# Attention weights of the whole prompt turned in 32 by 32 blocks on VectorE and put in place by SBUF transfers on two queues

## The chip, the cores and the metric

The kernel runs on one core of a Trainium2 chip. The metric is the device time of one execution in microseconds, lower is better. Every run is timed on the chip, and one more execution is recorded by the hardware profiler; all rows shown here come from that one.

## What is computed

The reference is one step of an encoder layer over a prompt of 2048 tokens and eight sample streams of 16 tokens each. One input projection feeds three branches (a gated convolution, a gated linear recurrence, an attention), and each branch goes through its slice of `w_branch`, is merged by gates and goes through `w_out`. The change touches the attention of the prompt alone. It has 8 heads of 64 channels and takes 128 queries at a time:

```python
def sb_attend(q, k, v, q_pos, k_pos):
    z = jnp.einsum('bqhd,bkhd->bhqk', qf, kf) * (1.0 / math.sqrt(SB_DH))
    causal = (k_pos[None, :] < q_pos[:, None])[None, None]
    log_1mb = jnp.where(causal, jax.nn.log_sigmoid(-z), 0.0)
    rest = lax.cumsum(log_1mb, axis=3, reverse=True) - log_1mb
    A = jnp.where(causal, jnp.exp(jax.nn.log_sigmoid(z) + rest), 0.0)
    return jnp.einsum('bhqk,bkhd->bqhd', A, vf)
```

A weight is the sigmoid of its own score times the product of (1 - sigmoid) over all keys between it and the query. The last product sums over keys, so the weights, which come out with queries on the partitions, have to be turned: keys on the partitions, queries along the row.

## The kernel before

Everything is float32 or a pair of float32 parts. The work has three stages. In the first (up to about 1340 us of the profile) the input projection of token groups 0 and 1 runs (matmuls L710 and L721), with the recurrence and the attention of the samples beside it. In the second (about 1340 to 2155 us) the projection of the third token group runs with the first part of the prompt's attention beside it. In the third (from about 2155 us) the branches are projected and merged (`bjob`, matmul L1440, the product with a gate on VectorE at L1446 and L1448, the sum at L1449), the output projection follows (`ojob`, L1471), and the rest of the prompt's attention runs beside that, up to about 2770 us.

The attention is a generator. It is advanced by a budget: each piece of foreground work names its cost in microseconds, that cost times a rate (0.65 in the second stage, 1.0 in the third) is credited, and every `yield` of the attention spends some of it. The merge of a group of 512 tokens calls `bg.drain(gi)` before it loads the attention's output, so what is left of that group's attention is then traced without foreground work between. The framework lays out each engine's queue from this order, and an instruction may be put ahead of one traced earlier; once laid out, each queue is worked off strictly in order.

The queries are taken in four blocks of 512 (`QBLOCKS`), the heads in four pairs. For a pair the keys are swept in segments of 512 from the newest to the oldest, once per head of the pair (`e` is 0 or 1). One such segment of one head is here called a sweep; there are 80. A sweep has four steps, one for each 128 queries (`i` from 0 to 3), 320 steps in all. A step is: two matmuls into `z` (L329, L330), two sigmoids on ScalarE (L333, L335) into `sn` and `sp`, a running product over the keys on VectorE (the scan, L342) into `pr`, and `sp` times `pr` (L347), which is the weight.

Three steps later (`DEPTH`) the helper `transposed` turns the weights: up to four 128 by 128 transposes on TensorE against the identity (L310) into the PSUM tile `tp`, and a copy by ScalarE (L311) into `aT`. When both heads of a segment are turned, `accumulate` adds `Vt` times `aT` into `pv` (16 matmuls, L359). After the last segment of a pair `store` multiplies by a gate (L366), splits the result into two parts and writes them to `OX` in DRAM (L182), from where the merge reads them (`load_o`, L1410).

`load_step` brings the keys `Kt` (two buffers) and the values `Vt` (two buffers). There is one buffer of `aT`, three of `sn`, four of `sp`, two of `pr`. All plain transfers are issued by SyncE (`nc.sync`), whose queue also carries the weights (`w`, `wst`: L208, L201), the gates of the merge (L1432, two buffers) and all stores.

## Time and profile before

| | us |
|---|---|
| median of 3 runs | 2874.01 |
| lowest and highest | 2873.08, 2874.37 |
| the profiled execution | 2876.11 |
| its span, first to last instruction | 2873.2 |

The granted TensorE clock was 1.0 throughout. The page gives busy time by engine, the chain of work that ended last, and groups of instructions: line, engine, operation, output and input, shape, count, then busy time and mean duration in ns, then the idle time of the engine just before them and what ended it. PE is TensorE's matmuls, PEld its weight loads, DVE is VectorE, ACT ScalarE, POOL GpSimd, SPq SyncE's queue of transfers. The view by windows gives the busy time and the number of instructions of each engine in a stretch, then the granted clock, the busy share of the 16 DMA engines and what they moved in GB/s. A TensorE that is listed as busy is not always at its peak, since matmuls are pipelined and their ends are modelled. The rows themselves stand in the prediction.

### The profile page before, as it was taken

Reading aid. Unit: us, or ns where it says so; the run is one execution under the profiler, and the core shown is the slowest. Engines: PE = TensorE matmul, PEld = TensorE weight load, DVE = VectorE, ACT = ScalarE, POOL = GpSimd, SP = SyncE. Lnnn points to the kernel's source line nnn. Section 1 sums busy time; section 2 is a strip of 40 time slices with the busy share of each in tenths; the row PEclk is TensorE's granted clock in tenths of the full one; section 3 lists DMA queues with packets and bytes.
Section 4 is the critical chain, followed back from the end, with each engine's and each line's share of the span. In section 5 each row is a group of like instructions: output and inputs, shape, how many; then the busy total and the mean of one; then the engine's idle time right before and its main releaser. Section 6 shows DMA issues by size and latency. Waiting matters only on the chain.

```text
span 2873.2 us, 51723 instructions
## 1 busy us (share of the span) xinstructions
PE 2853.0 (99%) x19479; PEld 2662.3 (93%) x19479; DVE 1546.5 (54%) x3304; ACT 1018.7 (35%) x2375; POOL 331.8 (12%) x802
## 2 busy tenths in 40 slices
PE   9999999999999999999999999999999999999999
PEld 9999999999999999999999999999998888787888
DVE  5454635641344442545434747557485876867743
ACT  4333222242233332213334444434444444544420
POOL 3110000111200000001323111111010011010100
PEclk9999999999999999999999999999999999999999
DMA  8887777777678887746766454544447877878876
GB/s 306 305 276 247 231 241 244 231 243 243 212 249 266 276 265 243 243 167 192 237 215 202 146 173 136 173 139 151 144 145 238 286 234 239 266 250 266 271 250 210
DMA packets 370475, 649.76 MB, mean 226 GB/s; under 512 B 33481, under 2 KB 246306, under 8 KB 339506
## 3 DMA queue, kind: packets, MB, share of 16 engines
q1 hardware_dynamic: 369458, 644.36, 68.2%
q8 instruction: 154, 2.52, 0.4%
q0 software_dynamic: 768, 2.10, 0.2%
q14 instruction: 95, 0.78, 0.1%
HBM read 447.06 MB, written 199.27 MB: 225 GB/s over the span
## 4 chain that ended last, share of the span: by engine, by line
PE 76%; DVE 2%; DMA 2%; issue 1%; ACT 0%; POOL 0%; SPq 0%; DVEq 0%; POOLq 0%; ACTq 0%
PE acc L710 33%; PE acc L721 10%; PE acc L1440 9%; PE acc L1471 6%; PE pv L359 4%; PE tp L310 4%; PE z L330 2%; PE z L329 2%; PE z L1039 1%; PE tp L458 1%; DMA gate<-GM 1%; PE pv L522 1%; PE z L476 0%; PE hg L1086 0%; PE hg L826 0%
## 5 line engine op out<-in xcount | busy, mean ns | idle before, releaser
L710 PE MATMUL acc<-hx,w 128*128 128x384 f32 (+1 forms) x6816 | 1251.8, 333 | 0.1
L710 PEld LDWEIGHTS acc<-hx,w 128*128 128x128 f32 x6816 | 1106.5, 188 | 21.9 <-issue 15.2
L721 PE MATMUL acc<-w,hx 128*128 128x256 f32 x2544 | 328.6, 284 | 1.8 <-DVE hx L176 0.9
L342 DVE TENSOR_TENSOR_SCAN pr<-snb,carry 128x513 f32<-128x513 f32 x192 | 246.5, 1284 | 153.3 <-ACT snb L333 151.7
L721 PEld LDWEIGHTS acc<-w,hx 128*128 128x128 f32 x2544 | 310.9, 188 | 5.0 <-DVE hx L176 1.7
L311 ACT COPY aT<-tp 128x512 f32<-128x512 f32 (+2 forms) x320 | 167.6, 524 | 375.2 <-PE tp L310 361.3
L710 PE MATMUL acc<-hx,wst 128*128 128x384 f32 x1248 | 247.2, 344 | 0.0
L1440 PE MATMUL acc<-o,w 128*128 128x512 f32 (+2 forms) x1080 | 234.7, 363 | 1.8 <-DMA o<-OX 1.8
L333 ACT ACTIVATE snb<-z 128x512 f32<-128x512 f32 (+2 forms) x320 | 172.4, 539 | 144.5 <-PE z L330 140.4
L710 PEld LDWEIGHTS acc<-hx,wst 128*128 128x128 f32 x1248 | 215.4, 188 | 6.4 <-issue 3.7
L1440 PEld LDWEIGHTS acc<-o,w 128*128 128x128 f32 x1080 | 185.1, 188 | 33.8 <-issue 5.3
L347 DVE TENSOR_TENSOR sp<-sp,pr 128x512 f32<-128x512 f32 (+2 forms) x320 | 195.3, 611 | 29.2 <-POOL sp L338 3.7
L342 DVE TENSOR_TENSOR_SCAN pr<-snb,one 128x129 f32<-128x129 f32 (+3 forms) x128 | 114.4, 894 | 123.9 <-POOL snb L338 123.6
L310 PE MATMUL tp<-idf,sp 128*128 128x128 f32 x1088 | 171.3, 273 | 2.5 <-ACT aT L311 1.5
L335 ACT ACTIVATE sp<-z 128x512 f32<-128x512 f32 (+2 forms) x320 | 171.5, 536 | 0.0
L1471 PE MATMUL acc<-w,mh 128*128 128x256 f32 x816 | 161.2, 285 | 1.0 <-DVE yt L1479 0.8
L1176 ACT ACTIVATE gm<-acc 128x384 f32<-128x384 f32 (+1 forms) x144 | 68.2, 474 | 230.4 <-PE acc L710 197.5
L310 PEld LDWEIGHTS tp<-idf,sp 128*128 128x128 f32 x1088 | 131.8, 141 | 19.3 <-issue 4.4
L176 DVE TENSOR_TENSOR w<-wst,w 128x1024 fp32r<-128x1024 f32 x72 | 88.1, 1223 | 110.7 <-ACT w L175 107.9
L1471 PEld LDWEIGHTS acc<-w,mh 128*128 128x128 f32 x816 | 131.0, 188 | 7.2 <-issue 4.2
L329 PE MATMUL z<-Kt,Q 128*128 128x512 f32 (+2 forms) x320 | 128.8, 403 | 0.3 <-ACT sp L335 0.2
L359 PE MATMUL pv<-aT,Vt 128*64 128x512 f32 (+3 forms) x640 | 128.1, 535 | 0.0
(299 smaller groups left out, 3570.1 us busy)
## 6 DMA issues: line engine op xcount, KB each, us to landing
w<-W SPq DMA_DIRECT2D x168, 1024.0 KB, 6.0
W<-w SPq DMA_DIRECT2D x72, 1024.0 KB, 5.0
wst<-W SPq DMA_DIRECT2D x112, 512.0 KB, 5.1
wst<-in_w_in_dram SPq DMA_DIRECT2D x72, 512.0 KB, 5.1
GM<-gm SPq DMA_DIRECT2D x120, 192.0 KB, 3.7
W<-mwp SPq DMA_DIRECT2D x40, 512.0 KB, 4.2
Kt<-KT SPq DMA_DIRECT2D x160, 128.0 KB, 3.1
o<-OX SPq DMA_DIRECT2D x72, 256.0 KB, 4.7
```

Source lines behind the costliest of these rows:

```text
L310: nc.tensor.transpose(tp[:, j * P:(j + 1) * P], sp[:, j * P:(j + 1) * P], idf)
L311: nc.scalar.copy(aT[:, e, 0:nb, i * P:(i + 1) * P], tp[:, :w].rearrange("p (b q) -> p b q", q=P))
L329: nc.tensor.matmul(z[:, :w], Q1[:, i * P:(i + 1) * P], Kt[:, :w], start=True, stop=False)
L333: nc.scalar.activation(sn[:, 512 - w:512], z[:, :w], AF.Sigmoid, scale=-0.125)
L335: nc.scalar.activation(sp[:, :w], z[:, :w], AF.Sigmoid, scale=0.125)
L342: nc.vector.tensor_tensor_scan(pr[:, 512 - w:513][:, ::-1], s_in, s_in, one if diag else carry[e][i], ALU.mult, ALU.bypass)
L347: nc.vector.tensor_tensor(sp[:, :w], sp[:, :w], pr[:, 513 - w:513], ALU.mult)
L359: nc.tensor.matmul(pv[64 * e:64 * e + 64, c0:n], Vt[:, j, e], aT[:, e, j, c0:n], start=first and j == 0, stop=last and j == nb - 1, skip_g ...
L710: nc.tensor.matmul(acc[:, :n], w[0][a][:, k], hT[b][:, k, :n], start=k == 0 and i == 0, stop=k == KB - 1 and i == 2)
L721: nc.tensor.matmul(acc[:, :256], hT[b][:, k, ti * P:(ti + 1) * P], w[k // 4][a][:, k % 4], start=k == 0 and i == 0, stop=k == KB - 1 and i ...
L1440: nc.tensor.matmul(acc[:, :n], w[0][a][:, k, dd * P:(dd + 1) * P], box[x][b][:, k, sl], start=k == 0 and i == 0, stop=k == 3 and i == 2)
L1471: nc.tensor.matmul(acc[:, :256], box["l" if b else "h"][:, k, ti * P:(ti + 1) * P], w[k // 4][a][:, k % 4], start=k == 0 and i == 0, stop= ...
```

## The change

The transposes on TensorE and the copies behind them are no longer called: `by_blocks` is set from the start and again before the third stage, so every sweep takes `turned_blocks`. One VectorE instruction per step turns each 32 by 32 block of the weights in its place, into a tile `T` of which there is one buffer, cleared once by GpSimd. After the last step of a sweep 16 transfers from SBUF to SBUF move the blocks to their partitions: each takes 32 partitions, and of each partition 16 runs of 32 values, in four runs of 512 bytes (64 KB in all). Eight are issued by SyncE and eight by ScalarE. They copy whole sweeps, so that blocks right of the diagonal go along. `aT` has a new order, in which the columns for `accumulate` are groups of 32 with a step of 128 values.

`accumulate` of a segment is held back in `pending` until the second step of the next segment's first sweep; at the end of a block of 512 queries it is held back by a `yield 5.0`. To make room, `sn` has two buffers in place of three, `Vt` one in place of two (its load moves behind the third step of the second head's sweep), and the tiles `ot` and `oth` of `store` share the two buffers of `pr`; the load of `ot` moves into the last `accumulate`.

```diff
-        for i in range(3):
+        for i in range(2):
             s = at.tile([P, 513], F32, name=f"snb{i}", bufs=1)
...
+        turned_.append(at.tile([P, 4, 4, 4, 32], F32, name="T", bufs=1))
+        nc.gpsimd.memset(turned_[0], 0.0)
...
-            nc.scalar.copy(aT[:, e, 0:nb, i * P:(i + 1) * P], tp[:, :w].rearrange("p (b q) -> p b q", q=P))
+            nc.scalar.copy(aT[:, e, i, :, 0:nb], tp[:, :w].rearrange("p (b a q) -> p a b q", a=4, q=32))
+
+        def turned_blocks(i, e, w, sp, aT):
+
+            T = turned_[0]
+            nc.vector.transpose(T[:, i, :, 0:w // P].rearrange("p c b q -> p b c q"),
+                                sp[:, :w].rearrange("p (b c q) -> p b c q", c=4, q=32))
+            if i == nq - 1:
+                for a in range(4):
+                    for c in range(4):
+                        queue_ = nc.scalar if (a + c) % 2 else nc.sync
+                        queue_.dma_start(aT[32 * c:32 * c + 32, e, :, a], T[32 * a:32 * a + 32, :, c])
...
-                aT = at.tile([P, 2, 4, 512], F32, tag="aT", name="aT", bufs=1)
+                aT = at.tile([P, 2, 4, 4, 4, 32], F32, tag="aT", name="aT", bufs=1)
+                turn_ = turned_blocks if by_blocks[0] else transposed
...
-                queue.append((True, lambda i=i, e=e, w=w, sp=sp, aT=aT: transposed(i, e, w, sp, aT)))
+                queue.append((True, lambda i=i, e=e, w=w, sp=sp, aT=aT, f=turn_: f(i, e, w, sp, aT)))
+                if e == 0 and i == 1:
+
+                    queue.extend(pending)
+                    pending.clear()
+                if e == 1 and i == 2:
+                    Vt = at.tile([P, 4, 2, 64], F32, tag="Vt", name="Vt", bufs=1)
+                    nc.sync.dma_start(Vt[:, :nb], VV[(1 + b0) * P:(1 + b1) * P, 2 * pair:2 * pair + 2].rearrange(
+                        "(b p) e c -> p b e c", p=P))
...
+                if last:
+                    gate.append(at.tile([P, 513], F32, tag="pr", name="ot", bufs=2))
+                    nc.sync.dma_start(gate[0][:, :n], SZ[pair][:, q0:q0 + n])
...
-                        nc.tensor.matmul(pv[64 * e:64 * e + 64, c0:n], Vt[:, j, e], aT[:, e, j, c0:n],
+                        nc.tensor.matmul(pv[64 * e:64 * e + 64, c0:n], Vt[:, j, e],
+                                         aT[:, e, c0 // P:nq, :, j].rearrange("p i a q -> p (i a) q"),
...
-            th = at.tile([P, 512], F32, tag="oth", name="oth", bufs=1)
+            th = at.tile([P, 513], F32, tag="pr", name="oth", bufs=2)
...
         yield from shorten(0)
+        if pending:
+            yield 5.0
+            queue.extend(pending)
+            pending.clear()
+            yield from shorten(0)
```

More of the change, by code (lines that the diff above doesn't have):

```diff
@@ L241, in trunk @@
     snb = []
+    turned_ = []
+    by_blocks = [True]
+    pending = []
     turn = [0]
@@ L317, in attn_pair @@
             load_step(m + 1)
-            if m == m1 - 1:
-                gate.append(at.tile([P, 512], F32, tag="ot", name="ot", bufs=1))
-                nc.sync.dma_start(gate[0][:, :n], SZ[pair][:, q0:q0 + n])
-            Q1, Q2, Kt, Vt = held[m]
+            Q1, Q2, Kt = held[m]
             nb = b1 - b0
@@ L324, in attn_pair @@
             if e == 0:
-                aT = at.tile([P, 2, 4, 512], F32, tag="aT", name="aT", bufs=1)
+                aT = at.tile([P, 2, 4, 4, 4, 32], F32, tag="aT", name="aT", bufs=1)
+                turn_ = turned_blocks if by_blocks[0] else transposed
+                if not by_blocks[0]:
+                    queue.extend(pending)
+                    pending.clear()
             for i in range(nq):
@@ L348, in attn_pair, with accumulate @@
                 yield 1.7 * w / 512
-                queue.append((True, lambda i=i, e=e, w=w, sp=sp, aT=aT: transposed(i, e, w, sp, aT)))
+                queue.append((True, lambda i=i, e=e, w=w, sp=sp, aT=aT, f=turn_: f(i, e, w, sp, aT)))
[6 more added lines that the diff above has]
+                        "(b p) e c -> p b e c", p=P))
                 yield from shorten(DEPTH)
-            def accumulate(nb=nb, diag=diag, first=si == 0, last=last, Vt=Vt, aT=aT):
+            def accumulate(nb=nb, diag=diag, first=si == 0, last=last, Vt=Vt if e else None, aT=aT):
                 if first:
                     box.append(ps_pv())
+                if last:
+                    gate.append(at.tile([P, 513], F32, tag="pr", name="ot", bufs=2))
+                    nc.sync.dma_start(gate[0][:, :n], SZ[pair][:, q0:q0 + n])
                 pv = box[0]
@@ L366, in store @@
             nc.vector.tensor_tensor(t[:, :n], box[0][:, :n], t[:, :n], ALU.mult)
-            th = at.tile([P, 512], F32, tag="oth", name="oth", bufs=1)
+            th = at.tile([P, 513], F32, tag="pr", name="oth", bufs=2)
             store_parts(OX[2, pair], slice(q0, q0 + n), t[:, :n], th[:, :n])
-        queue.append((False, store))
+        (pending if turn_ is turned_blocks else queue).append((False, store))
     queue = []
@@ L386, in attention @@
         yield from shorten(0)
+        if pending:
+            yield 5.0
+            queue.extend(pending)
+            pending.clear()
+            yield from shorten(0)
     def sample_attention():
```

11 lines of the change are left out of this document (3 added, 8 removed).

## The prediction

> **What bounds the kernel now.** I read the page's busy times first, then its chain.
>
> ```profile
> PE 2853.0 (99%) x19479; PEld 2662.3 (93%) x19479; DVE 1546.5 (54%) x3304; ACT 1018.7 (35%) x2375; POOL 331.8 (12%) x802
> ...
> PE 76%; DVE 2%; DMA 2%; issue 1%; ACT 0%; POOL 0%; SPq 0%; DVEq 0%; POOLq 0%; ACTq 0%
> PE acc L710 33%; PE acc L721 10%; PE acc L1440 9%; PE acc L1471 6%; PE pv L359 4%; PE tp L310 4%; PE z L330 2%; PE z L329 2%; PE z L1039 1%; PE tp L458 1%; DMA gate<-GM 1%; PE pv L522 1%; PE z L476 0%; PE hg L1086 0%; PE hg L826 0%
> ```
>
> TensorE is busy from end to end, and the chain lies on it. The transposes that the change removes (L310) hold 4% of it; no other engine has a share worth removing. But these are averages, so I asked the windows view for the stages.
>
> ```profile
> 0.00:1340.00 1340.00, 1331.64 (x9761) 1301.24 (x9762) 608.12 (x1618) 416.71 (x1003) 125.64 (x262) 1.00 0.75 246
> 1340.00:2155.00 815.00, 811.73 (x5277) 761.87 (x5276) 472.86 (x1028) 325.85 (x816) 147.47 (x341) 1.00 0.53 171
> 2155.00:2770.00 615.00, 610.98 (x3806) 509.65 (x3805) 429.92 (x600) 270.63 (x548) 58.71 (x199) 1.00 0.77 253
> 2770.00:2873.00 103.00, 98.62 (x643) 89.55 (x641) 35.57 (x60) 5.47 (x9) 0.00 (x0) 1.00 0.69 237
> ```
>
> The columns are PE, PEld, DVE, ACT, POOL, the clock, the share of the transfer engines and GB/s. The prompt's attention runs in the second and third rows. In the second, VectorE is busy 473 of 815 us and the transfer engines 0.53: room everywhere but on TensorE. In the third, VectorE is at 430 of 615 (0.70) and the transfer engines at 0.77. TensorE is still the bound there, but the two resources that the change loads are the next ones.
>
> **What is removed.** The chain asked stage by stage (second, then third):
>
> ```profile
> by line: PE acc L710 54.0%; PE acc L721 16.9%; PE pv L359 6.3%; PE tp L310 6.2%; PE z L330 3.5%; PE z L329 3.3%; PE z L1039 2.0%; DVE pr L342 0.8%; PE hg L826 0.6%; PE hg L1086 0.6%; DMA xt<-in_x_prompt_dram 0.6%; DMA Q<-QT 0.6%; PE tp L108
> by line: PE acc L1440 38.9%; PE acc L1471 23.1%; PE pv L359 11.8%; PE tp L310 10.4%; PE z L330 5.5%; PE z L329 5.4%; PE acc L710 1.6%; DMA o<-OX 0.8%; DMA GM<-gm 0.6%; issue 0.5%; DVE sp L347 0.2%; DVE mp L1449 0.1%; SPq L1410 0.1%; ACT snb
> ```
>
> 6.2% of 815 us is 50.5 us, 10.4% of 615 us is 64.0 us: 114.5 us of TensorE's path go if nothing takes their place. The busy time of the group is larger, since neighbours overlap in it:
>
> ```profile
> L311 ACT COPY aT<-tp 128x512 f32<-128x512 f32 (+2 forms) x320 | 167.6, 524 | 375.2 <-PE tp L310 361.3
> L310 PE MATMUL tp<-idf,sp 128*128 128x128 f32 x1088 | 171.3, 273 | 2.5 <-ACT aT L311 1.5 <-DVE sp L347 1.0
> ```
>
> 171.3 us is the upper bound of the saving, 114.5 the value I take. The copies on ScalarE (167.6 us) were hidden behind TensorE and are worth nothing by themselves.
>
> **What is added on VectorE.** 320 block transposes of one input and one output. No such instruction is in the trace. Nearest is the product of the same shapes (L347), an upper neighbour the scan (L342); per stage, product first:
>
> ```profile
> 1340.00:2155.00 815.00, 89.21 (x155) 1.00 0.53 171
> 2155.00:2770.00 615.00, 106.13 (x166) 1.00 0.77 253
> 1340.00:2155.00 815.00, 164.66 (x155) 1.00 0.53 171
> 2155.00:2770.00 615.00, 196.22 (x165) 1.00 0.77 253
> ```
>
> I take the product: 89 us in the second stage, 106 in the third; the bound above is the scan, 165 and 196, and a bound below half the product, 45 and 53, as it reads one input in place of two. VectorE then stands at 473 + 89 = 562 of 815, which hides, and at 430 + 106 = 536 us in the third stage. Without the transposes TensorE would need 615 - 64 = 551 us there, so VectorE would be at 97%. It cannot be hidden as before: with a short wait VectorE is the bound. Where foreground work on it is thickest (third branch of the merge) it has no gap already:
>
> ```profile
> 2473.32 1.28 DVE L342 TENSOR_TENSOR_SCAN pr<-snb,carry 128x513 f32<-128x513 f32 x1
> 2474.52 0.66 DVE L1448 TENSOR_TENSOR gate<-acc,gate 128x512 f32<-128x512 f32 x1
> 2475.10 0.68 DVE L347 TENSOR_TENSOR sp<-sp,pr 128x512 f32<-128x512 f32 x1
> 2475.70 0.68 DVE L1449 TENSOR_TENSOR mp<-mp,gate 128x512 f32<-128x512 f32 x1
> 2476.37 1.29 DVE L342 TENSOR_TENSOR_SCAN pr<-snb,carry 128x513 f32<-128x513 f32 x1
> 2477.57 0.67 DVE L176 TENSOR_TENSOR ml<-mp,mh 128x512 fp32r<-128x512 f32 x1
> ```
>
> The Trainium skill ("VectorE: DVE Perf Modes", section on the three transpose paths) gives 311 ns for a 128 by 128 bf16 turned on VectorE; four of them, as an estimate, make 1.24 us for a full step. No run here shows it yet; it would put the transposes at the scan's price, the fourth case below.
>
> **The wait that is added.** `T` has one buffer and all 16 transfers of a sweep read all of it, so the first transpose of the next sweep waits until the last has landed. Rows for issue and landing:
>
> ```profile
> 2472.43 2.34 SPq L1410 DMA_DIRECT2D o<-OX  x5
> Kt<-KT SPq DMA_DIRECT2D x160, 128.0 KB, 3.1
> OX<-ot SPq DMA_DIRECT2D x16, 256.0 KB, 2.0
> ```
>
> Five issues in a row take 2.34 us, 0.45 each; eight on each queue take 3.6 us. ScalarE's issues are not in the trace; I take SyncE's price, between nothing and twice that. Landing lies between 2.0 (a store) and 3.1 us (a load). So `T` is free 5.6 to 6.7 us after the sweep's last transpose. The next one comes one step later, in the third stage 615 us / 166 steps = 3.7 us. The wait is 1.9 to 3.0 us, per sweep (166 / 4 = 41.5 sweeps in the third stage, 155 / 4 = 39 in the second). Queued behind it on VectorE are the next scan and, in the merge, the products that empty `acc` (three buffers), for which TensorE waits. I take 1.9: 41.5 x 1.9 = 79 us, and 536 + 79 = 615 us. **The third stage then takes as long as before**, with VectorE in TensorE's place. The 64 us are given back.
>
> In the second stage a wait of 1.9 us x 39 = 74 us leaves VectorE at 636 of 765 us, so it mostly hides. What does not hide are the bursts: ScalarE waits for the last transpose and then issues for 3.6 us, and behind it stand the copies that empty `acc` (two buffers); SyncE does the same, and weights, keys and stores stand behind it. Between 0 and 1 us per sweep, I take 0.25: 10 us. Lifting the copies off ScalarE gives room for the 39 x 3.6 = 140 us of issues.
>
> **Transfers.** 16 x 64 KB is 1.05 MB per sweep, 43.5 MB in the third stage beside 253 GB/s x 615 us = 155.6 MB. The largest sustained flow of the page is 306 GB/s:
>
> ```profile
> GB/s 306 305 276 247 231 241 244 231 243 243 212 249 266 276 265 243 243 167 192 237 215 202 146 173 136 173 139 151 144 145 238 286 234 239 266 250 266 271 250 210
> ```
>
> 199.1 MB at 306 GB/s are 651 us, more than 615; but nothing in the trace says that 306 is a limit (TensorE was busy throughout there), and traffic inside SBUF leaves HBM alone. I cost it at nothing beyond the forecast's 615 us (324 GB/s) and keep 651 as a rival. The Trainium skill ("DMA: Bandwidth & Descriptors", section Measured) gives 0.95 us for 64 KB; 16 of them one after the other, as an estimate, are 15.2 us of the 14.8 us that a sweep takes. The rows above have larger transfers issued 0.45 us apart and landing in 2 to 5 us, so they overlap, and I do not take it.
>
> **Smaller edits.** `accumulate` waits for the landings, but is held back at least two steps (7 us), which covers 5.6 to 6.7: nothing. Its matmuls read groups of 32 in place of a plain row; no row has such an operand, so between nothing and as much again as it costs (4% of the chain, 115 us); I take nothing, as the count of columns is the same. The scans wait for `pr` while `ot` and `oth` hold it, 16 times, and the second `sn` is nearer; hidden behind foreground matmuls, up to 3 us each if not (48 us). Clearing `T` falls where GpSimd is idle.
>
> **The end.** The last attention output is read straight after it is written:
>
> ```profile
> 2764.73 4.39 PE L359 MATMUL pv<-aT,Vt 128*64 128x512 f32 x16
> 2770.53 0.32 SPq L182 DMA_DIRECT2D OX<-oth  x1
> 2773.56 0.88 SPq L1410 DMA_DIRECT2D o<-OX  x2
> ```
>
> So the last drain decides. Four `yield 5.0` put the attention 20 us of budget further back, and the last `accumulate` now waits 5.6 to 6.7 us for its transfers with nothing traced between. Merge matmuls that are left over cover part; I take 12 us, between 0 and 25.
>
> **The sum**, against the profiled execution of 2876.1 us (2.9 of it outside its span, 2.1 above the median of 2874.0): 2876.1 - 50.5 + 10 + 0 (third stage: -64 + 64) + 12 = 2847.6 us for the profiled execution, and 2.1 less, **2845.5 us**, for the median. I predict 2846.
>
> **The rivals.**
> First, *everything hides*: the wait on `T` falls into VectorE's gaps and only the end costs: third stage 551 us, 2876 - 114.5 + 10 + 12 = 2784. For it: the framework may put other work ahead of a waiting transpose. Against: the 97%.
> Second, *slower, by VectorE's wait on `T` in the third stage*: with landings like the loads' 3.1 us or later under load, the wait is 3 us and more: 536 + 41.5 x 3.0 = 661, +46 us, 2894; at 4 us 702 and 2935. It decides from 28 us over 615, a wait of 2.6 us. For it: VectorE without a gap; gates with two buffers, whose loads queue behind SyncE's bursts and which VectorE needs in order. Against: half of the stage (output projection, first branch) loads VectorE less.
> Third, *the transfers bound the third stage*: 651 us, +36: 2884. For it: share 0.77 before. Against: above.
> Fourth, *the transpose costs a scan*: 430 + 196 + 79 = 705 us, +90: 2938.
> Fifth, *no change*: the second stage's 40 us are eaten by bursts of 1 us and the drain: about 2874.
>
> **How the numbers follow.** Forecast (2800 to 2868) 0.45; everything hides (under 2800) 0.10; no change (2868 to 2880) 0.09; slower by the wait or the transfers (2880 to 2935) 0.29; dearer transposes or worse (above) 0.07. About 0.2% is what a measurement of this kernel can tell from no change. Faster 0.55, same 0.09, slower 0.36. The likeliest case's own range is 2800 to 2868; to leave out no more than 0.2 the range runs from 2782 to 2932.
>
> **What would show it.** Right: L310 and L311 gone; the second stage 40 us shorter; in the third VectorE above 0.85 busy, with waits of VectorE for landings into `aT` of about 2 us per sweep, and a chain with VectorE or transfers in it; the transposes near 0.69 us for 512 columns. Wrong: a third stage near 551 us (everything hid), one over 640 us (waits or transfers), transposes of 1.2 us, L359 dearer, or transfers that land in more than 4 us.

## The result, and the profile after

| | before | after |
|---|---|---|
| median, us | 2874.19 | 3169.43 |
| lowest to highest of 4 runs each | 2873.08 to 2875.68 | 3157.35 to 3179.72 |
| the profiled execution | 2876.11 | 3168.90 |
| its span | 2873.2 | 3167.2 |
| mean granted TensorE clock | 1.000 | 0.956 |

The changed kernel takes 1.1025 times as long, with a 95% interval of 1.0986 to 1.1065: 295 us slower. The forecast was 28 us faster, and the time lies far above its range.

From the page of the kernel after: busy time by engine, the granted clock in 40 slices, and the two groups of instructions that the change adds or alters.

```profile
PE 2902.5 (92%) x18391; PEld 2625.5 (83%) x18391; DVE 1691.7 (53%) x3623; ACT 874.3 (28%) x2055; POOL 337.2 (11%) x803
...
PEclk9999999999999999999999999999988888888899
...
L316 DVE STREAM_TRANSPOSE T<-sp 128x512 f32<-128x512 f32 (+2 forms) x320 | 186.1, 608 | 49.2 <-DMA aT<-T 47.5
L382 PE MATMUL pv<-aT,Vt 128*64 128x512 f32 (+3 forms) x640 | 166.1, 553 | 31.1 <-DMA aT<-T 29.9
```

No engine is full any more. TensorE went from 99% to 92%, VectorE stands at 53%. TensorE's instructions fell by 1088, the transposes, and yet its busy time rose by 50 us: in the last third the granted clock drops, and each matmul lasts longer. So the time was not lost to more work. It was lost to waiting, and to the lower clock that goes with it.

Where it was lost is read from two instructions that bound the stages: the first matmul of the merge on `o`, with which the third stage begins, and the last matmul of `accumulate`, with which the attention ends. The view by source line gives the first and the last start of each, here for before and for after:

```profile
L1440 PE MATMUL acc<-o,w x1080: 274/392/483, 2182.9 to 2816.5; 128*128 128x512 f32 x108, 128*128 128x384 f32 x38, 128*128 128x256 f32 x34
L359 PE MATMUL pv<-aT,Vt x640: 272/592/644, 1385.9 to 2768.5; 128*64 128x512 f32 x112, 128*64 128x384 f32 x16, 128*64 128x256 f32 x16, 128*64 128x128 f32 x16
...
L1470 PE MATMUL acc<-o,w x1080: 274/392/796, 2195.0 to 3109.6; 128*128 128x512 f32 x108, 128*128 128x384 f32 x36, 128*128 128x256 f32 x36
L382 PE MATMUL pv<-aT,Vt x640: 272/592/1116, 1395.7 to 3078.9; 128*64 128x512 f32 x112, 128*64 128x256 f32 x26, 128*64 128x384 f32 x16, 128*64 128x128 f32 x6
```

The second stage thus ends 12.1 us later (2195.0 - 2182.9), the third takes 883.9 in place of 585.6 us, 298.3 more, and what comes after it is 16.4 us shorter (88.3 in place of 104.7 of the span). That makes the 294 us between the spans. **The third stage holds nearly all of the loss.** The shorter end is no gain of its own: of the 2528 matmuls of the merge and the output projection 376 start after the attention's last matmul in the trace of after, where 496 did before, so 120 of them have moved into the third stage.

The windows view of after for the second and the third stage, columns as in the prediction:

```profile
1340.00:2195.00 855.00, 806.16 (x4878) 733.27 (x4878) 537.11 (x1189) 259.66 (x677) 142.51 (x343) 0.99 0.71 211
2195.00:3075.00 880.00, 681.46 (x3227) 519.37 (x3228) 514.75 (x766) 190.45 (x365) 66.81 (x197) 0.86 0.76 226
```

In the third stage TensorE is busy for 77% at a clock of 0.86, VectorE for 58%, the transfer engines for 0.76 at 226 GB/s, less than the 253 GB/s before. Nothing is saturated. Both parts of the loss can be read against the run without transfers that is told below (`no_transfers`: 563.3 us busy of 588 for 3206 matmuls): TensorE's matmuls take 118 us longer in after, and it stands idle for 174 us more (198.5 in place of 24.7). What VectorE and ScalarE wait for in that window (engine, line, what released it; then us in total, times, longest):

```profile
ACT snb L345 <- DMA aT<-T: 87.1, 15, 9.4
ACT sp L347 <- DMA aT<-T: 80.1, 11, 9.7
DVE gate L1478 <- DMA gate<-GM: 46.9, 25, 5.4
DVE mp L1476 <- DMA gate<-GM: 35.4, 14, 7.7
DVE T L316 <- DMA aT<-T: 32.0, 15, 3.8
PE pv L382 <- DMA aT<-T: 28.0, 15, 3.7
ACT sp L347 <- DMA o<-OX: 24.8, 3, 10.3
DVE yt L1509 <- DMA xr<-in_x_prompt_dram: 21.0, 14, 4.9
DVE yt L1509 <- DMA out_dram<-yt: 18.6, 8, 5.5
```

The wait that the prediction priced, VectorE's for `T` (L316), is one of the small ones: 32 us. Larger are waits for things that the change did not touch: the gates (82 us in two rows) and the rows of `x` for the output, all of them loads by SyncE. And ScalarE waits 167 us for landings in `aT` before its sigmoids (two rows), though a sigmoid reads and writes nothing of `aT`, and 25 us for `o`, which it does not read either. Such a row says that something else, which stood ahead of the sigmoid in ScalarE's queue, had to wait. A stretch of the timeline shows it (start, duration, engine, operation; in brackets the idle time before and what ended it):

```profile
2862.57 7.81 SPq L322 DMA_DIRECT2D aT<-T  x8
...
2864.15 3.92 ACTq L322 DMA_DIRECT2D aT<-T  x4
...
2868.11 0.62 ACT L175 CAST mh<-mp 128x512 fp32r<-128x512 f32 x1 [3.35 <-DMA aT<-T]
...
2870.48 0.53 SPq L1462 DMA_DIRECT2D gate<-GM  x1
```

SyncE needs 7.8 us for its eight issues, waits between them included, and the load of the next gate stands behind them until 2870.5. ScalarE needs 3.9 us for four, and a cast (L175) that makes the merge's operand for TensorE stands behind those. The view of `aT` has the issues by queue (duration min, median and max in ns, first and last start):

```profile
L322 ACTq DMA_DIRECT2D aT<-T x640: 592/612/1935, 1353.6 to 3072.8; - x160
L322 SPq DMA_DIRECT2D aT<-T x640: 585/603/2244, 1355.2 to 3073.4; - x160
```

So one of these issues takes 0.6 us, 640 times on each of two queues that have other work: 640 x 0.603 = 386 us of SyncE and 392 us of ScalarE, to replace 168 us of copies on ScalarE.

### The profile page after: what moved, and what is told of

It is laid out like the page before. It is cut to its first block, busy times and chain, and to the rows that moved or that the text cites. A ratio compares the mean times of both kernels' runs of the same rounds, so it can differ in the third digit from the quotient of the medians.

```text
span 3167.2 us, 51219 instructions
## 1 busy us (share of the span) xinstructions
PE 2902.5 (92%) x18391; PEld 2625.5 (83%) x18391; DVE 1691.7 (53%) x3623; ACT 874.3 (28%) x2055; POOL 337.2 (11%) x803
## 5 line engine op out<-in xcount | busy, mean ns | idle before, releaser
L1470 PE MATMUL acc<-o,w 128*128 128x512 f32 (+2 forms) x1080 | 256.2, 389 | 46.6 <-DVE gate L1478 18.6
L1470 PEld LDWEIGHTS acc<-o,w 128*128 128x128 f32 x1080 | 201.3, 207 | 95.5 <-DVE gate L1478 24.4
L316 DVE STREAM_TRANSPOSE T<-sp 128x512 f32<-128x512 f32 (+2 forms) x320 | 186.1, 608 | 49.2 <-DMA aT<-T 47.5
L1501 PE MATMUL acc<-w,mh 128*128 128x256 f32 x816 | 180.5, 311 | 34.5 <-DVE yt L1509 16.6
L382 PE MATMUL pv<-aT,Vt 128*64 128x512 f32 (+3 forms) x640 | 166.1, 553 | 31.1 <-DMA aT<-T 29.9
L1501 PEld LDWEIGHTS acc<-w,mh 128*128 128x128 f32 x816 | 149.0, 216 | 43.0 <-DVE yt L1509 19.2
L341 PEld LDWEIGHTS z<-Kt,Q 128*128 128x128 f32 x320 | 62.3, 195 | 105.6 <-ACT sp L347 83.9
L382 PEld LDWEIGHTS pv<-aT,Vt 128*64 128x64 f32 x640 | 53.0, 139 | 105.1 <-issue 89.7
```

What stands on the lines that cost most here:

```text
L316: nc.vector.transpose(T[:, i, :, 0:w // P].rearrange("p c b q -> p b c q"), sp[:, :w].rearrange("p (b c q) -> p b c q", c=4, q=32))
L341: nc.tensor.matmul(z[:, :w], Q1[:, i * P:(i + 1) * P], Kt[:, :w], start=True, stop=False)
L382: nc.tensor.matmul(pv[64 * e:64 * e + 64, c0:n], Vt[:, j, e], aT[:, e, c0 // P:nq, :, j].rearrange("p i a q -> p (i a) q"), start=first an ...
L1470: nc.tensor.matmul(acc[:, :n], w[0][a][:, k, dd * P:(dd + 1) * P], box[x][b][:, k, sl], start=k == 0 and i == 0, stop=k == 3 and i == 2)
L1501: nc.tensor.matmul(acc[:, :256], box["l" if b else "h"][:, k, ti * P:(ti + 1) * P], w[k // 4][a][:, k % 4], start=k == 0 and i == 0, stop= ...
```

## The experiments

The theories:
- **T wait**: VectorE waits for the landings before it writes `T` again (the prediction's second rival).
- **Bytes**: the transfers fill the transfer engines (its third).
- **Loop**: the transfers wait until `accumulate` has read `aT`, `accumulate` and all behind it on TensorE wait for the transfers.
- **Issues**: 16 issues per sweep hold SyncE's and ScalarE's queues, and the loads, casts and sigmoids behind them come late.

Each time is that of one execution; the kernel before, run beside them on the same chip, took 2872 to 2876 us. The four runs of after spread over 22 us, so smaller differences among the slow kernels are not told apart. The table has all kernels, in the order in which they are told. "Third stage" is from the first merge matmul on `o` to the last matmul of `accumulate`, read as above.

| kernel | us | third stage begins | its length | granted clock, whole run |
|---|---|---|---|---|
| before | 2876.1 | 2182.9 | 585.6 | 1.000 |
| after | 3168.9 | 2195.0 | 883.9 | 0.956 |
| buffers_only | 2877.5 | 2185.1 | 587.1 | 0.999 |
| no_transfers | 2808.9 | 2136.3 | 588.0 | 0.997 |
| second_only | 2913.5 | 2197.9 | 621.4 | 0.994 |
| third_only | 3139.8 | 2186.6 | 854.0 | 0.960 |
| const_source | 3144.0 | 2168.2 | 883.8 | 0.957 |
| quarter_bytes | 3114.9 | 2193.2 | 827.6 | 0.965 |
| quarter_count | 2899.2 | 2143.2 | 671.2 | 0.988 |
| sp_pool | 3088.3 | 2186.0 | 812.6 | 0.967 |
| sp_queue | 3335.8 | 2299.4 | 945.5 | 0.941 |
| pool_queue | 3288.4 | 2277.6 | 932.2 | 0.947 |
| by_dram | 3127.2 | 2168.6 | 880.5 | 0.966 |
| by_dram_second | 2891.9 | 2173.5 | 624.1 | 0.995 |
| sink | 3146.9 | 2182.8 | 855.3 | 0.960 |
| const_sink | 3103.6 | 2178.0 | 814.0 | 0.960 |
| const_sink_pool | 2969.3 | 2212.4 | 670.3 | 0.978 |
| const_sink_act | 2885.3 | 2212.4 | 587.1 | 0.991 |
| const_sink_sp | 3008.1 | 2153.3 | 753.5 | 0.975 |
| rows | 3142.4 | 2193.5 | 858.0 | 0.957 |

### What the side edits cost, and what could be won

`buffers_only` keeps all the buffer edits and the new order of `aT`, but turns the weights on TensorE as before.

```diff
-    by_blocks = [True]
+    by_blocks = [False]
...
-    by_blocks[0] = True
```

> The weights are turned by TensorE throughout as before, with everything else of the change: two sn buffers, one Vt, ot and oth in the buffers of pr, aT in the new order. If the loss comes from the transfers or the wait on T: within 15 us of 2874. If it comes from the smaller buffers: over 3000. If the new order of aT makes the accumulate matmuls dearer: 20 to 115 us over 2874, with their mean above 535 ns.

2877.5 beside 2875.4 us: two sigmoid buffers, one `Vt`, shared `pr` tiles and the strided operand of `accumulate` cost about 2 us together. They are not the cause.

`no_transfers` turns the blocks into `T` as in the change, but moves nothing; `accumulate` reads a cleared `aT`.

```diff
...
-                for a in range(4):
-                    for c in range(4):
-                        queue_ = nc.scalar if (a + c) % 2 else nc.sync
-                        queue_.dma_start(aT[32 * c:32 * c + 32, e, :, a], T[32 * a:32 * a + 32, :, c])
+                pass
...
-                aT = at.tile([P, 2, 4, 4, 4, 32], F32, tag="aT", name="aT", bufs=1)
+                aT = turned_[1]
```

> Leaves the 16 transfers of every sweep out (accumulate reads a tile of zeros, so the attention's output is left out of the result); the block transposes on VectorE, their buffers and the held back accumulate stay. If the wait on T, the issues or the bytes of the transfers are the cause of the loss (three theories that this run doesn't tell apart), TensorE's saving shows and the time is 2780 to 2830 us, with the clock back at 1.0. If VectorE's 186 us of transposes alone fill the third stage, 2850 to 2950. If the smaller buffers are the cause, over 3000.

2808.9 us, 66.5 us below the run beside it. Its windows, second stage and third:

```profile
1340.00:2136.00 796.00, 784.03 (x4890) 726.05 (x4889) 549.38 (x1196) 263.02 (x680) 138.04 (x343) 1.00 0.55 178
2136.00:2724.00 588.00, 563.30 (x3206) 455.00 (x3206) 502.43 (x760) 181.94 (x360) 62.26 (x195) 0.99 0.81 266
```

The second stage ends 46.6 us earlier than before (2182.9 - 2136.3). The third takes 588 us, as long as before, though it has fewer matmuls and no landing in `aT` to wait for: VectorE is busy for 502 of 588 us there (0.85), TensorE for 563 (0.96), and the chain has both. What follows it is 21.9 us shorter (82.8 in place of 104.7), with 102 fewer matmuls of the merge and output projection left in it. Third stage and end together are thus 19.5 us shorter (670.8 in place of 690.3). So all that the transposes could give is these 66 us, 46.6 of them in the second stage, and **the transfers take away 360 us** (3168.9 - 2808.9). The experiments that follow ask how.

### One stage at a time

`second_only` turns by blocks in the second stage alone, `third_only` in the third alone: of the two switches shown above one is set to `False`, ahead of the third stage or at the start.

> Turned in blocks in the second stage, by TensorE in the third. The second stage of the changed kernel took 855 us in place of 815: if the stages are independent, 2874 + 40 = 2914, 2890 to 2940. If the second stage's loss came from attention that the third left over or the other way round, the sum of this run's and the next one's excess differs from 295 us by more than 40.

> Turned by TensorE in the second stage, in blocks in the third, which took 880 us in place of 615 in the changed kernel: if the stages are independent, 2874 + 255 = 3129, 3090 to 3160, with a clock of about 0.86 in the third stage. My forecast's own wait on T (1.9 to 3.0 us a sweep) would give 2874 to 2925.

+38 us (2913.5 beside 2875.4) and +264 us (3139.8): together 302, the change's own loss of 295 within a few us. The stages lose on their own. Nor does the second stage alone win anything: in `second_only` its end is at 2197.9 in place of 2182.9, where without transfers it was 46.6 us early. It also leaves work behind: 164 scans in place of 157 start in the third stage, 8 of its block transposes among the work left over, and that stage is 36 us longer than before.

### Is it the wait on T, the bytes, or the count?

`const_source` lets the transfers read a constant tile, so that VectorE never waits for them before it writes `T`. `quarter_bytes` keeps the 16 transfers and moves one of a sweep's four steps (16 KB in place of 64). `quarter_count` issues 4 of the 16, of 64 KB each. In both of these `aT` is one tile that is cleared at the start, as in `no_transfers`.

```diff
 const_source
-  queue_.dma_start(aT[32 * c:32 * c + 32, e, :, a], T[32 * a:32 * a + 32, :, c])
+  queue_.dma_start(aT[32 * c:32 * c + 32, e, :, a], g_bc[32 * a:32 * a + 32, 0:512].rearrange("p (i r) -> p i r", i=4))
 quarter_bytes
+  queue_.dma_start(aT[32 * c:32 * c + 32, e, 0, a], T[32 * a:32 * a + 32, 0, c])
 quarter_count
-                    for c in range(4):
-                        queue_ = nc.scalar if (a + c) % 2 else nc.sync
+                    for c in (a,):
+                        queue_ = nc.scalar if a % 2 else nc.sync
```

> All 16 transfers per sweep, full size, into aT as before, but read from a constant tile in place of T; VectorE still turns every step into T, so T is never read, no transpose waits for a landing and no issue for a transpose (the attention's weights are left out of the result). Theory of the wait on T, my forecast's: 2810 to 2860, since the wait is gone. Issue theory (issues take ScalarE's and SyncE's time, and each waits for an earlier transfer's completion): still over 3000. Bytes theory: over 3000.

> All 16 transfers per sweep are issued, but each moves one run of 512 bytes per partition in place of four (16 KB in place of 64 KB); the rest of aT stays zero, so three quarters of the attention's weights are left out. Without any transfers the kernel took 2809 us, with all 3169: 360 us to explain. Bytes theory (the transfer engines are full): a quarter of 360, about 2900. Issue theory (number of transfers, their place in the queues and their completion): 3080 to 3170. Theory of the wait on T: landings are a little shorter, 3050 to 3150.

> Four full transfers of 64 KB per sweep, two on each queue, in place of 16; the other blocks of aT stay zero, so three quarters of the weights are left out. Same bytes as in the run with a quarter of the bytes. Bytes theory: the same time as that run, about 2900. Issue theory: 2820 to 2890, clearly under that run. Wait on T: T is free about 1.2 + 2.6 = 3.8 us after the last transpose, so hardly a wait: 2810 to 2850.

3144.0, 3114.9 and 2899.2 us. Without the T wait 25 us come back of 360, hardly more than the runs of after differ among themselves, with a quarter of the bytes 54, with a quarter of the issues 270 (9 us less than the issue theory had expected at the least). **The price goes mainly by the transfer, not by the byte, and VectorE's wait is a small part of it.** The third stage makes a near straight line of it. The transposes L316 in its window are 168, so 42 sweeps of four; with 0, 4 and 16 transfers per sweep it takes 588.0, 671.2 and 883.9 us. That is 83.2 / 168 = 0.50 us per transfer for the first four, and 295.9 / 672 = 0.44 us over all 16, beside an issue of 0.60 us.

### Other queues

`sp_pool` issues ScalarE's eight on GpSimd, `sp_queue` all 16 on SyncE, `pool_queue` all on GpSimd.

```diff
-                        queue_ = nc.scalar if (a + c) % 2 else nc.sync
+                        queue_ = nc.gpsimd if (a + c) % 2 else nc.sync    # sp_pool
+                        queue_ = nc.sync                                  # sp_queue
+                        queue_ = nc.gpsimd                                # pool_queue
```

> The changed kernel with ScalarE's eight transfers per sweep issued by GpSimd in place of ScalarE. Issue theory: ScalarE's queue is free and GpSimd's transfers complete on their own, 2880 to 3000, if GpSimd needs no more than about 1 us for each issue (8 per sweep of 14 us); if it needs more, T is free later and the time rises to 3100 or more. Wait on T: 3100 or more in any case, as the last landing isn't earlier. Bytes: unchanged, 3150 to 3190.

> All 16 transfers per sweep issued by SyncE, none by ScalarE. If ScalarE's blocked queue (sigmoids behind issues) is the larger part: 2950 to 3080, though SyncE then issues 9.6 us per sweep. If SyncE's blocked queue (gates, weights and keys behind issues) is the larger part: over 3200.

> The changed kernel with all 16 transfers per sweep issued by GpSimd: SyncE's and ScalarE's queues are as without them, and GpSimd's transfers have completion semaphores of their own. The issues took 0.55 us each there, 8.8 us per sweep of 14, so T is free only about 12 us after the last transpose and the wait on T grows. If SyncE's and ScalarE's blocked queues are what costs: 2900 to 3020. If the length of the path from T to accumulate is what costs: over 3150.

3088.3, 3335.8 and 3288.4 us. With ScalarE freed 81 us come back, which lies between the two ranges that had been expected (2880 to 3000, and 3100 or more). SyncE alone is worst. `pool_queue` is a miss: it frees both engines and was to come out at 2900 to 3020 us. Its waits in the third stage show what replaced the old ones:

```profile
ACT sp L347 <- DVE T L316: 400.6, 49, 21.1
...
PE pv L382 <- DMA aT<-T: 160.4, 27, 11.3
...
POOL aT L322 <- PE pv L382: 93.3, 14, 12.9
POOL aT L322 <- DVE T L316: 90.0, 20, 15.2
```

With one queue the last of 16 issues comes at least 16 x 0.55 = 8.8 us after the first (the view of `sp_pool` has 0.55 us for one on GpSimd), `accumulate` and the next `T` wait for it, and GpSimd, standing at an issue that waits for `accumulate` (93 us), holds up the masks and carries of the next scan: in the same view the scans wait 60 us for these two (37.2 and 22.5). Here the loop does seem to cost. This left two theories, loop and issues, for the change itself.

### Fewer and larger transfers by way of DRAM

`by_dram` writes `T` to DRAM in one transfer of SyncE and reads it back in four of GpSimd; `by_dram_second` does so in the second stage alone and transposes on TensorE in the third.

```diff
+                TD = dram.tile([P, 4, 4, 4, 32], F32, tag="TD", name="TD", bufs=2)
+                nc.sync.dma_start(TD, T)
+                for c in range(4):
+                    nc.gpsimd.dma_start(aT[32 * c:32 * c + 32, e].rearrange("p i a j q -> p i a (j q)"),
+                                 TD[:, :, c].rearrange("(a r) i b q -> r i a (b q)", a=4))
```

> In place of 16 transfers inside SBUF, five per sweep through DRAM: T is written whole by SyncE (1 MB in rows of 8 KB), and four reads by GpSimd bring it back in runs of 512 bytes. Twice the bytes, a third of the issues, one of them on SyncE, and T waits for one landing alone. Issue theory: 2830 to 2920. Bytes theory: the third stage carries 2 x 43.5 MB more, over 3050.

> The same five transfers per sweep in the second stage alone, TensorE's transposes in the third, where VectorE would become the bound even without transfers (588 us before, 590 without transfers). The second stage saved 47 us without transfers: 2874 - 47 + up to 30 for the five issues and the longer path = 2830 to 2860, faster than both kernels. Bytes theory: 2890 or more.

3127.2 and 2891.9 us: neither is in the range of the issue theory, both are in that of the bytes. The windows row of `by_dram`'s third stage, the row of its reads (KB each, us to landing), the issue of its write and the longest wait of GpSimd's issues there:

```profile
2168.00:3049.00 881.00, 690.12 (x3291) 515.99 (x3293) 510.24 (x772) 188.94 (x363) 212.70 (x367) 0.88 0.94 285
...
aT<-TD POOLq DMA_DIRECT2D x320, 256.0 KB, 7.6
...
L320 SPq DMA_DIRECT2D TD<-T x80: 319/325/752, 1355.8 to 3011.4; - x80
...
POOL aT L322 <- DMA TD<-T: 206.3, 20, 19.7
```

The transfer engines stand at 0.94, and a read lands after 7.6 us. But a share of 0.94 is not by itself the reason: `const_sink_pool`, told below, has it too in a third stage of 670 us. The path also got longer, as a read waits for the write to land: GpSimd stood 206 us at such issues in that stage. Which of the two costs, bytes or path, was not separated, so these two runs say little about the change's own loss.

### Cutting the loop

`sink` lets `accumulate` read a constant tile in place of `aT`: nothing on TensorE waits for a transfer. `const_sink` does that and lets the transfers read a constant tile as well: no instruction waits for a transfer's data and no transfer for an instruction; what is left are the issues, their bytes and their completions. `const_sink_pool` is `const_sink` with all issues on GpSimd.

```diff
 sink, const_sink, const_sink_pool
-                                         aT[:, e, c0 // P:nq, :, j].rearrange("p i a q -> p (i a) q"),
+                                         g_bc[:, c0:n],
```

> Leaves out: accumulate reads a constant tile in place of aT, so nothing on TensorE waits for the 16 transfers of a sweep and the transfers wait for no matmul; they still read T, and VectorE still waits for them before it writes T again. If the cost is the closed loop (b): about 2830 to 2900 us, that is 270 us and more come back. If it is the issues on ScalarE and SyncE (a): 3050 to 3150 us, near the 3144 us of the constant source.

> Leaves out: the transfers carry a constant tile to aT and accumulate reads a constant tile, so no instruction waits for a transfer's data and no transfer for an instruction; only the 16 issues of a sweep, their bytes and their completions are left, at the same places of ScalarE's and SyncE's order. (b) the closed loop: 2810 to 2860 us, as without any transfer (2809). (a) the issues by themselves: 3050 us or more. In between (2900 to 3000): both, in the share that it shows.

> As const_sink, with all 16 issues on GpSimd in place of ScalarE and SyncE. By (a), the issues hold ScalarE's and SyncE's queues: 2810 to 2860 us, as these are free of them, and TensorE waits little for GpSimd. If the transfers cost by what they do in the transfer engines, whoever issues them: within 40 us of const_sink.

3146.9 and 3103.6 us: the loop theory, which had 2830 to 2900 and 2810 to 2860, falls. **Of the 360 us, 295 are there with nothing but the issues** (3103.6 - 2808.9). (These issues still carry their bytes, and each has a landing that is reported.) Closing either half of the loop adds some 40 (to 3144.0 with `accumulate` waiting, to 3146.9 with `T`), both halves 65. ScalarE in `const_sink` (timeline):

```profile
2420.28 5.45 ACTq L322 DMA_DIRECT2D aT<-g_bc  x5
2425.82 0.60 ACT L345 ACTIVATE snb<-z 128x512 f32<-128x512 f32 x1 [5.91 <-DMA aT<-g_bc]
```

The sigmoid has no tie to these transfers; it waits 5.9 us because five issues stand ahead of it, from the first to the last 5.45 us. Each of the five takes 0.59 to 0.61 us in its own record, 3.0 together; in the 2.5 us between them an issue waits in its turn. With all issues on GpSimd the price is 160 us over `no_transfers` in place of 295, 134 less, and yet 2969.3 lies well above the 2810 to 2860 expected. That it matters which queue is held is likely, but this run doesn't show it alone: 886 of its 1280 issues start before the third stage, where `const_sink` has 665, so that 394 are left for the third stage in place of 608.

### Whose queue?

`const_sink_act` and `const_sink_sp` are `const_sink` with only one queue's eight transfers. In `rows` the tiles are laid out so that a transfer moves one run of 2 KB per partition in place of four of 512 bytes.

```diff
 const_sink_act
+                        if (a + c) % 2 == 0:
+                            continue
+                        queue_ = nc.scalar
 const_sink_sp
+                        if (a + c) % 2:
+                            continue
+                        queue_ = nc.sync
 rows
...
-            nc.vector.transpose(T[:, i, :, 0:w // P].rearrange("p c b q -> p b c q"),
+            nc.vector.transpose(T[:, :, i, 0:w // P].rearrange("p c b q -> p b c q"),
...
-                        queue_.dma_start(aT[32 * c:32 * c + 32, e, :, a], T[32 * a:32 * a + 32, :, c])
+                        queue_.dma_start(aT[32 * c:32 * c + 32, e, a], T[32 * a:32 * a + 32, c])
...
```

> As const_sink (constant source, accumulate reads a constant), with only ScalarE's 8 transfers of a sweep; SyncE's 8 are left out. If the cost is each queue's own issue time, the two halves add up to const_sink's 295 us over 2809, with the larger part here, since the sigmoids stand behind these issues: about 2980 to 3010 us, and 2880 to 2910 for SyncE's half. If it is the shared limit on transfers under way, each half costs much less than half: 2820 to 2870 us here, and the two halves together under 100 us.

> As const_sink, with only SyncE's 8 transfers of a sweep; ScalarE's 8 are left out. Own issue time: 2880 to 2910 us, the rest of the 295 us. Shared limit on transfers under way: 2820 to 2870 us.

> Leaves nothing out. T and aT are laid out so that a transfer moves one run of 2 KB per partition in place of four of 512 bytes, the count and the bytes unchanged. If the pieces of a transfer set the price (its issue or its landing): issues under 0.5 us, landings nearer 2.0 us, and 3000 us or less. If the price is per transfer: issues of 0.6 us as before and 3110 to 3180 us.

3008.1 us with SyncE's half, 2885.3 with ScalarE's: 199 and 76 us over `no_transfers`, 275 of `const_sink`'s 295 together. SyncE's half is by far the dearer; I had expected the opposite. But the two are not alike, as the view of `aT` in `const_sink_act` shows:

```profile
L324 ACTq DMA_DIRECT2D aT<-g_bc x640: 592/612/2267, 1332.7 to 2213.9; - x160
```

With nothing to wait for, the framework put all but 2 of ScalarE's 640 issues ahead of the third stage, and the second stage gets 76 us longer (2212.4 - 2136.3); the third takes 587 us. So this run says what ScalarE's issues cost in the second stage when there are twice as many, and nothing of the third. There `const_sink`, with 304 of ScalarE's issues beside SyncE's, takes 60.5 us more than SyncE's alone (814.0 - 753.5).

`const_sink_sp` spreads its issues over both stages like the change (1355 to 2908 us). It costs 17 us in the second, **165 us in the third stage** (753.5 - 588.0) and 17 behind it. The chain of work there:

```profile
2690.27 0.70 DVE mp L1481
2690.99 0.32 SPq L1464
...
2691.36 0.64 SPq L324
...
2695.95 0.60 SPq L324
2696.59 0.59 SPq L201
...
2698.26 0.50 SPq L293
...
2700.60 0.43 SPq L1442
2701.07 8.15 DMA o<-OX
2709.28 5.43 DMA gate<-GM
```

SyncE itself lies on the chain: from 2691.4 to 2696.5 us it issues eight transfers into `aT`, behind them come weights (L201), keys (L293) and `o` (L1442). Then the issue of a gate stands until an `o` has landed (8.15 us), with which it shares no data, and the landing of the gate ends the wait at 2714.7. So the issues of the burst are 5.2 us of this piece, and the larger part are landings that follow late. VectorE's waits in that stage:

```profile
DVE gate L1480 <- DMA gate<-GM: 34.9, 14, 8.3
...
DVE yt L1511 <- DMA xr<-in_x_prompt_dram: 26.7, 13, 5.1
...
DVE mp L1478 <- DMA gate<-GM: 17.4, 9, 5.0
DVE yt L1511 <- DMA xr<-in_x_sample_dram: 14.9, 2, 7.9
```

Summed over all its rows of that view, VectorE waits in the third stage for transfers 7.6 us before, 32.6 in `no_transfers`, 104.6 in `const_sink_sp`, 173.9 in `const_sink` and 177.1 in after; the stage takes 586, 588, 754, 814 and 884 us in these. The two grow together. Behind each such wait stand the scans, the products that empty `acc`, and then TensorE.

`rows` took 3142.4 us, 15 below the lowest of the change's runs. A quarter of the pieces does not make the issue shorter in the median:

```profile
L322 ACTq DMA_DIRECT2D aT<-T x640: 513/601/2274, 1353.4 to 3044.9; - x160
L322 SPq DMA_DIRECT2D aT<-T x640: 507/589/2033, 1354.9 to 3045.5; - x160
```

Nor did a quarter of the bytes (medians of 601 and 588 ns in `quarter_bytes`). So an issue into `aT` takes 0.6 us in all three layouts. That is not the price of every issue: the write of `T` in `by_dram`, 1 MB, takes SyncE 0.33 us (its row above), and in the trace of before the median is 0.34 us for a `w` of 1 MB and 0.59 us for a `Kt` of 128 KB. It does not go by the size; what it goes by was not tested.

**What stays open.** SyncE and ScalarE share eight completion semaphores, which the program gives to their transfers by turns (the records of `const_sink` name the same eight for both queues, and eight others for GpSimd). A transfer is issued only when the one before it with the same semaphore has landed. So the two queues wait for each other's transfers without sharing data. In the third stage of `const_sink` the loads and stores that SyncE issues beside the transfers stood 117.7 us in all until an `aT` had landed; the two largest rows are `o` and the gates:

```profile
SPq L1440 <- DMA aT<-g_bc: 49.9, 22, 6.6
SPq L1462 <- DMA aT<-g_bc: 22.9, 10, 7.3
```

In `const_sink_sp` there are no such waits. There SyncE's issues into `aT` take 195 us in the third stage, and stand 39 us more until some other transfer has landed, for the 165 us that the stage is longer. So with one queue the time of the issues is the larger part; with both, how much of the 295 us is this sharing and how much the issues' own time was not separated. Moving issues to GpSimd (`sp_pool`, `const_sink_pool`) undoes the sharing too: in `sp_pool` the same sum is 1.7 us. Its 81 us are thus the worth of both. `const_sink_act` was to tell them apart, and its issues moved. Apart from `no_transfers` no kernel tried is faster than the one before. With 4 transfers per sweep the second stage did end 39.7 us early (2143.2), but those were a quarter of the transfers that are needed.

## Why the prediction was wrong

**What held.** The transposes and copies went. Their removal is worth 46.6 us in the second stage (`no_transfers`), where 50.5 were read from the chain. The block transposes cost what the product costs, by the windows view of after, second and third stage:

```profile
1340.00:2195.00 855.00, 83.92 (x152) 0.99 0.71 211
2195.00:3075.00 880.00, 102.16 (x168) 0.86 0.76 226
```

84 and 102 us stand beside 89 and 106. The Trainium skill ("VectorE: DVE Perf Modes", section on the three transpose paths) would have made it the scan's price by its 311 ns for 128 by 128 in bf16; the trace does not agree, at 0.69 us for four such blocks of float32. That the third stage gives most of the gain back once VectorE is loaded held as well, and even without a wait for landings: in `no_transfers` it takes 588 us, with VectorE at 0.85, and with what follows it 19.5 us less than before, of 64 that were read from the chain. (The sum had needed 79 us of waits to give back all of it.) The buffers and the strided operand, costed at nothing, took about 2 us (`buffers_only`).

**The step that failed** is the one on the bursts in "The wait that is added": "Between 0 and 1 us per sweep, I take 0.25: 10 us". It saw that "weights, keys and stores stand behind" SyncE's issues, but priced that for the second stage alone and by guess. The second stage lost 58.7 us against `no_transfers` (2195.0 - 2136.3), 1.5 us for each of 39 sweeps, and gave back all it had won. In the third stage the sum had no term for it at all: 536 us of work and 79 of waits on `T` filled VectorE, and SyncE's queue was not looked at. The runs showed 226 us for the issues alone there (814.0 - 588.0), 165 of them with SyncE's half, and some 70 more with the waits for the data. (226 and 165 hold what the issues wait for each other's landings, too.) I counted how long the eight issues would keep `T`, not what they keep from being issued.

**The second rival** had the right sign and named the place: gates "whose loads queue behind SyncE's bursts and which VectorE needs in order". But it put this down as support for a wait on `T`. That wait was worth about 25 us (`const_source`), so the rival's price, 46 to 87 us, came from the wrong mechanism and was far too small. Its threshold, a wait of 2.6 us, decided nothing.

**The transfers as a bound** (third rival): no. In the third stage the change moves fewer GB/s than the kernel before (226 beside 253), and a quarter of the bytes gave 54 of 360 us.

**Sizes.** An issue was priced at 0.45 us from `o<-OX` and took 0.60; landings in `aT` took 2.0 to 7.9 us with a median of 2.6, where 2.0 to 3.1 were assumed. The end, costed at +12, came out at -16, because 120 matmuls of the merge and output projection that stood there before are now done in the third stage; so this says nothing of the drain that the 12 us were for.

**What would have shown it beforehand**: to count SyncE's work in the third stage as that of any engine. In the trace of before SyncE issues 495 transfers between the two bounds of that stage, and these issues take 223 of 586 us; 336 more at 0.6 us are another 202 us, in bursts of 4.8 us in front of loads that had been issued just in time. In after the issues take 459 us of 884, so issuing alone did not fill the queue: the sum would have shown the danger, and not the 298 us.

## What to carry to other kernels

A transfer costs its issuing queue time that does not go by its bytes (here 0.6 us for 64 KB and for 16, and 0.33 us for a write of 1 MB), and an engine's queue is worked off in order; so price an edit that adds transfers by their number on each queue, and name every load, cast and activation that will stand behind a burst. A queue that only issues transfers is an engine with a busy time too: add up its issues by stage before and after, above all where the page lists it at 0% of the chain. Turning in blocks costs little in itself (186 us of VectorE for 320 tiles); it is the 16 moves per four tiles that made it dearer here than the transposes, even beside a TensorE that was the bound.

## What was not expected of the hardware

**The issue is not small beside the transfer.** The Trainium skill ("DMA: Bandwidth & Descriptors", section "Issuing engines are not separate DMA queues") says that issuing from several engines saves only the sequencer's time, "which is usually small relative to the DMA itself". Here an issue takes 0.60 us on SyncE and ScalarE and 0.55 on GpSimd beside 2.2 to 3.1 us of landing, and landings overlap while issues do not. So the trace does not agree that the issue is small, and the whole kernel became 199 us slower by eight of them per sweep on SyncE (`const_sink_sp`).

**Where TensorE waits more, its clock is lower.** Its granted clock was 1.0 throughout before, 0.99 in the third stage of `no_transfers`, 0.91 in that of `const_sink_sp` and 0.86 in that of after, where it is busy for 77%. The two went together in these runs; that the waits bring the clock down was not tested. In after the longer matmuls are 118 us of the third stage beside 174 us of idle time, so a busy time that rises while the instructions fall is worth a look at the clock.
